# Four of eight blocks of the second MLP product by Strassen's method, accumulators in pairs of banks, fixed product orders

## The chip, the cores and the metric

The kernel runs on one core of a Trainium2 chip. The metric is the device time of one execution in microseconds (us), as the median of several runs. TensorE multiplies matrices and writes its sums to PSUM banks (128 x 512 float32 each, eight of them); VectorE and ScalarE do elementwise work; SP and ScalarE issue the DMAs used here.

## The reference

Two decoder layers over 256 tokens of width 2048. Layer 0 mixes a gated short convolution with differential attention, layer 1 is forgetting attention; each is followed by an MLP with a squared ReLU of hidden width 8192:

```python
def _sqrelu_mlp(h, w1, w2):
    return jnp.square(jax.nn.relu(h @ w1)) @ w2

for l in range(DEPTH):
    h = _rmsnorm(x, norm1_g[l])
    x = x + mixer_l(h)            # layer 0: conv + diff attention; layer 1: forgetting attention
    h = _rmsnorm(x, norm2_g[l])
    x = x + _sqrelu_mlp(h, mlp_w1[l], mlp_w2[l])
```

## The kernel before

**Precision.** Each large product is computed from split operands. A float32 value is cast to a high part (`wh`, or `hi` of an activation, by ScalarE) and VectorE subtracts it from the value to get a low part (`wl`, `lo`). Three matmuls then stand for one product: high by high, high by low, low by high. `split_w` (L142) does this for a weight tile of 1 MB (`raw`, three buffers); `wh` and `wl` have three buffers each (`wspl`, L41).

**Projections.** `gemm` (L153) makes 256 tokens by 512 columns: two accumulators (token halves t), blocks of 512 rows of the weight. Within half a block 12 matmuls are issued in one of six written orders (`ORDERS`, L132), taken in turn. `proj` copies the result out on ScalarE; `out_proj` (L534) adds it to the residual with one VectorE addition for each t. After half a block `step` (L84) advances one generator of `pending`: normalisation, attention, the convolution and `setup` (L246), which loads small parameters on ScalarE's queue, the forget-gate weights `gw` (L260) last.

**The MLP.** `mlp` (L706) goes over four groups g of 2048 hidden units. `hidden` (L604) makes the first product of a group in eight calls of `gemm_t` (L544), 256 hidden units each, 64 matmuls, in one of four orders (`TORDERS`, L699). Its results are taken out later (`take`, L620, put into `late` and run by `flush`), squared, and stored as a pair for the second product. `gemm_pair` (L638) is the second product: it is called twice in a group, for columns n = 0, 1 and n = 2, 3, and each call goes through the eight pairs. A letter of `KINDS` says how a pair is multiplied with its 256 x 1024 block of the weight, seen as a 2 x 2 matrix of blocks:

- C, classical: 8 block products, 24 matmuls; the weight tile is split once.
- S, Strassen's method in Winograd's form: 7 block products, 21 matmuls. VectorE first makes sums of weight blocks (`T`, L650 to L654), and both three of the raw blocks and the four of `T` are split, which takes two of the `wspl` buffers. `PairS.fill` also makes sums of the hidden activations.

In a call, products go to eight PSUM banks: four accumulators (P2, Q3, Q4, X) that S and C share, and P1, Q5, P7, P6 that only S uses. One block behind the last S, those four are combined into `E` and added to the residual (L678 to L689). At the end of the call `final` (L692) adds the four accumulators to the residual, one VectorE operation each, run by the next `flush`. In the last group of the last layer each of the four also starts a store of its 256 KB part of the output.

**Order.** The order in which the engines get their instructions is not the written one: the framework places each instruction when it expects its data and its buffer to be ready, and so pulls instructions ahead of others. On an engine the order is then fixed. A tile of a pool is given again when all that used its buffer before is done.

Of the kernel before, what the change touches and what calls it, by code (L numbers as in the profile page):

```python
# [16 lines left out]
P = 128  # L17
# [9 lines left out]
def trunk_kernel(  # L27
# [18 lines left out]
    accp = ctx.enter_context(tc.tile_pool(name="accp", bufs=4, space=PSUM))  # L46
# [19 lines left out]
    nc.scalar.copy(g1, ps[:, :32])  # L66

# [42 lines left out]
    class ActT:  # L110
# [20 lines left out]

    ORDERS = [  # L132
        lambda kk: [(t, k, p) for t in range(2) for k in kk for p in (0, 1, 2)],
        lambda kk: [(t, k, p) for t in range(2) for k in kk for p in (0, 2, 1)],
        lambda kk: [(t, k, p) for t in range(2) for p in (0, 1, 2) for k in kk],
        lambda kk: [(t, k, p) for k in kk for t in range(2) for p in (0, 1, 2)],
        lambda kk: [(t, k, p) for k in kk for p in (0, 2, 1) for t in range(2)],
        lambda kk: [(t, k, p) for k in kk for p in (0, 1, 2) for t in range(2)],
    ]
    turn = [0, 0]  # L140

# [11 lines left out]
    def gemm(acts, w, c0, first=False):  # L153

        acc = []
        total = 4 * len(acts)
        i = 0
        for ai, a in enumerate(acts):
            raw = wraw.tile([P, 4, CW], F32, name="raw")
            src = w[a.row:a.row + CW, c0:c0 + CW].rearrange("(k p) n -> p k n", p=P)  # L160
            if first and ai == 0:
                for h in range(2):
                    nc.sync.dma_start(raw[:, 2 * h:2 * h + 2, :], src[:, 2 * h:2 * h + 2, :])
            else:
                nc.sync.dma_start(raw, src)
            wh, wl = split_w(raw, parts=2 if first else 1)
            if i == 0:
                flush()
                acc += [accp.tile([P, CW], F32, name="acc") for _ in range(2)]
            until(lambda: a.left <= 0)  # L170
            for h in range(2):
                kk = (2 * h, 2 * h + 1)
                seq = ORDERS[turn[0] % len(ORDERS)](kk)
                for j, (t, k, p) in enumerate(seq):
                    ts = slice(t * P, (t + 1) * P)
                    x = (a.lo if p == 2 else a.hi)[:, k, ts]
                    st = i + 2 * h == 0 and all(q[0] != t for q in seq[:j])
                    sp = i + 2 * h + 2 == total and all(q[0] != t for q in seq[j + 1:])
                    nc.tensor.matmul(acc[t], x, (wl if p == 1 else wh)[:, k, :], start=st, stop=sp)  # L179
                step()  # L180
            i += 4
        turn[0] += 1
        return acc
# [59 lines left out]
    gw = const.tile([P, KT, 16], F32, name="gw")  # L243
    gws = const.tile([P, GP], F32R, name="gws")

    def setup():  # L246
# [13 lines left out]
        nc.scalar.dma_start(gw, fox_w_in[0, :, 3 * D:3 * D + 16].rearrange("(k p) n -> p k n", p=P))  # L260
# [166 lines left out]
    def forget_gates(nm):  # L427

        wv = gws[:, :KT * 32].rearrange("p (k n) -> p k n", n=32)
# [104 lines left out]
    def out_proj(acts, w, nxt):  # L534

        for part in (acts[:-1], acts[-1:]):
            for n in range(NCH):
                acc = gemm(part, w, n * CW)
                for t in range(2):
                    nc.vector.tensor_tensor(xr[n][:, t, :], acc[t], xr[n][:, t, :], ALU.add)  # L540
                if len(part) == 1:
                    pending.append(nxt.chunk(n))

    def gemm_t(acts, w, c0):  # L544
# [3 lines left out]
        for c in range(2):  # L548
# [4 lines left out]
            if c == 0:  # L553
                flush()
                acc += [accp.tile([P, CW], F32, name="acc") for _ in range(2)]
            for h in range(2):
                a = acts[2 * c + h]
                until(lambda: a.left <= 0)
                for f, k, p in TORDERS[turn[1] % len(TORDERS)]:
# [13 lines left out]
    KINDS = "SCSCSCCC"  # L573
# [30 lines left out]
    def hidden(nm, w, c0):  # L604

        pairs, half = [], None
        for i, kind in enumerate(KINDS):
            acc = gemm_t(nm.acts, w, c0 + 2 * i * P)
            if kind == "S":
                p = PairS()  # L610
            elif half is not None:
                p, half = PairC(half), None
            elif "C" in KINDS[i + 1:]:
                t = actp.tile([P, 4, 2, 2 * P], F32R, name="act")
                p, half = PairC(t[:, :2]), t[:, 2:]
            else:
                p = PairC(qkv.tile([P, 2, 2, 2 * P], F32R, name="v"))
# [12 lines left out]
            turn[1] += 1  # L630
# [7 lines left out]
    def gemm_pair(pairs, w, r0, n, r2, done):  # L638
# [3 lines left out]
        for i, (kind, p) in enumerate(zip(KINDS, pairs)):  # L642
# [15 lines left out]
            if i == 0:  # L658
                flush()
                for nm in ("P2", "Q3", "Q4", "X"):  # L660
                    B[nm] = accp.tile([P, CW], F32, name="acc")
# [30 lines left out]
        def final():  # L692
            for bank, m, t in (("P2", n + 1, 0), ("Q3", n, 0), ("X", n, 1), ("Q4", n + 1, 1)):
                nc.vector.scalar_tensor_tensor(
                    xr[m][:, t, :], B[bank], r2[:, t:t + 1], xr[m][:, t, :], ALU.mult, ALU.add)
                done(1, m, t)
        late.append(final)

    TORDERS = [  # L699
        [(f, k, p) for f in range(2) for p in range(2) for k in range(4)],  # L700
        [(f, k, p) for p in range(2) for k in range(4) for f in range(2)],
        [(f, k, p) for p in range(2) for f in range(2) for k in range(4)],
        [(f, k, p) for f in range(2) for k2 in (0, 2) for p in range(2) for k in (k2, k2 + 1)],
    ]
# [97 lines left out]
```

## Time and profile before

| | |
|---|---|
| median of 3 runs | 2183.34 us (2182.51 to 2185.11) |
| profiled execution | 2183.53 us, its span 2181.8 us |
| TensorE busy | 2167.7 us, 10724 instructions |
| VectorE busy | 1541.1 us, 1572 instructions |
| ScalarE busy | 1049.5 us, 1099 instructions |
| read from HBM | 408.28 MB, 188 GB/s over the span |

How to read it: PE is TensorE's matmuls, PEld its weight loads, DVE is VectorE, ACT ScalarE, SP the engine that issues the weight loads; ACTq is ScalarE's queue of instructions. A matmul's row lasts longer than the distance to the next one, since they are pipelined. "<-" names what ended an idle time. L12 is line 12 of the kernel. The span is shorter than the time of the execution by what lies around it.

### The profile page before, as it was taken

How to read it: one execution, taken by the hardware profiler on the slowest of the kernel's cores; microseconds unless marked ns; L12 is line 12 of the kernel's file. 1: busy time of each engine (PE TensorE's matmuls, PEld its weight loads, DVE VectorE, ACT ScalarE, POOL GpSimd, SP SyncE). 2: the span in 40 equal slices, each digit the busy share in tenths (PEclk: the TensorE clock that was granted, in tenths of full speed). 3: DMA queues.
4: the chain of work that ended last, by engine and by line, in shares of the span. 5: the costliest groups of instructions: out<-in, count | busy, mean ns of one | idle time of the engine just before them, and what ended most of it. 6: DMA issues, size and time to landing. Idle time of an engine off the chain costs nothing.

```text
span 2181.8 us, 25989 instructions
## 1 busy us (share of the span) xinstructions
PE 2167.7 (99%) x10724; PEld 1821.4 (83%) x10724; DVE 1541.1 (71%) x1572; ACT 1049.5 (48%) x1099; POOL 17.0 (1%) x17
## 2 busy tenths in 40 slices
PE   8999999999999999999999999999999999999999
PEld 6887888888888888888888888888888888888887
DVE  5576655779768768867856565657797687687687
ACT  6465443544445444445554454445454444444453
POOL 0000000000000000000000000000000000000000
PEclk9999999999999999999999999999999999999999
DMA  7554555555755765665655555556556556656654
GB/s 257 174 174 155 175 191 193 175 172 194 222 182 175 229 191 178 211 193 176 211 173 189 188 176 173 183 174 181 166 205 219 179 181 221 191 186 209 189 189 153
DMA packets 245241, 412.08 MB, mean 189 GB/s; under 512 B 9367, under 2 KB 144770, under 8 KB 245122
## 3 DMA queue, kind: packets, MB, share of 16 engines
q1 hardware_dynamic: 237264, 405.84, 57.4%
q10 hardware_dynamic: 7858, 4.58, 0.7%
q8 instruction: 84, 1.38, 0.3%
q14 instruction: 35, 0.29, 0.0%
HBM read 408.28 MB, written 2.11 MB: 188 GB/s over the span
## 4 chain that ended last, share of the span: by engine, by line
PE 94%; DVE 3%; DMA 2%; ACT 1%; issue 0%; SPq 0%; ACTq 0%; DVEq 0%
PE acc L179 32%; PE acc L562 22%; PE acc L566 11%; PE acc L635 7%; PE acc L636 7%; PE acc L634 7%; PE tp L635 2%; PE tp L634 2%; PE tp L636 2%; DVE wl L150 1%; DMA raw<-in_mlp_w_dram 1%; PE tp L199 1%; ACT wh L149 0%; PE tp L320 0%; DVE qk L651 0%
## 5 line engine op out<-in xcount | busy, mean ns | idle before, releaser
L150 DVE TENSOR_TENSOR wl<-raw,wh 128x2048 fp32r<-128x2048 f32 (+2 forms) x388 | 853.7, 2202 | 507.5 <-ACT wh L149 507.2
L149 ACT CAST wh<-raw 128x2048 fp32r<-128x2048 f32 (+2 forms) x388 | 713.2, 1840 | 758.3 <-issue 249.7
L179 PE MATMUL acc<-wh,act 128*128 128x512 f32 x2048 | 624.2, 398 | 1.7 <-ACT wh L149 1.7
L562 PE MATMUL acc<-act,wh 128*128 128x512 f32 x2048 | 557.6, 394 | 0.0
L179 PEld LDWEIGHTS acc<-wh,act 128*128 128x128 f32 x2048 | 380.8, 189 | 79.3 <-ACT wh L149 2.1
L562 PEld LDWEIGHTS acc<-act,wh 128*128 128x128 f32 x2048 | 349.9, 189 | 45.7 <-DVE act L128 0.6
L179 PE MATMUL acc<-wl,act 128*128 128x512 f32 x1024 | 360.6, 392 | 2.8 <-DVE wl L150 2.8
L566 PEld LDWEIGHTS acc<-act,wl 128*128 128x128 f32 x2048 | 314.3, 189 | 43.4
L566 PE MATMUL acc<-act,wl 128*128 128x256 f32 x2048 | 324.7, 281 | 0.0
L635 PE MATMUL acc<-wl,act 128*128 128x512 f32 x656 | 256.3, 391 | 1.5 <-DVE wl L150 1.4
L636 PE MATMUL acc<-wh,act 128*128 128x512 f32 x656 | 255.3, 389 | 0.0
L634 PE MATMUL acc<-wh,act 128*128 128x512 f32 x656 | 251.5, 389 | 0.0
L179 PEld LDWEIGHTS acc<-wl,act 128*128 128x128 f32 x1024 | 193.0, 189 | 44.3 <-DVE wl L150 4.0
L635 PEld LDWEIGHTS acc<-wl,act 128*128 128x128 f32 x656 | 123.1, 188 | 30.1 <-DVE wl L150 4.7
L634 PEld LDWEIGHTS acc<-wh,act 128*128 128x128 f32 x656 | 123.2, 188 | 25.8
L636 PEld LDWEIGHTS acc<-wh,act 128*128 128x128 f32 x656 | 123.2, 188 | 25.3
L149 ACT CAST wh<-qk 128x2048 fp32r<-128x2048 f32 x48 | 91.9, 1914 | 105.0 <-DVE qk L654 69.6
L150 DVE TENSOR_TENSOR wl<-qk,wh 128x2048 fp32r<-128x2048 f32 x48 | 109.9, 2290 | 22.6 <-ACT wh L149 22.4
L624 ACT COPY qk<-acc 128x256 f32<-128x256 f32 x128 | 43.9, 369 | 73.4 <-PE acc L566 73.4
L635 PE MATMUL tp<-wl,act 128*128 128x512 f32 x192 | 74.8, 389 | 0.0
L634 PE MATMUL tp<-wh,act 128*128 128x512 f32 x192 | 74.7, 389 | 0.0
L636 PE MATMUL tp<-wh,act 128*128 128x512 f32 x192 | 74.7, 389 | 0.0
(171 smaller groups left out, 1424.2 us busy)
## 6 DMA issues: line engine op xcount, KB each, us to landing
raw<-in_mlp_w_dram SPq DMA_DIRECT2D x256, 1024.0 KB, 5.5
raw<-in_fox_w_in_dram SPq DMA_DIRECT2D x48, 1024.0 KB, 5.1
raw<-in_hyb_w_in_dram SPq DMA_DIRECT2D x47, 1024.0 KB, 5.1
raw<-in_hyb_w_out_dram SPq DMA_DIRECT2D x16, 1024.0 KB, 5.1
raw<-in_fox_w_out_dram SPq DMA_DIRECT2D x16, 1024.0 KB, 5.0
ob<-fcd ACTq DMA_DIRECT2D x4, 512.0 KB, 5.7
xr<-in_x_dram SPq DMA_DIRECT2D x3, 512.0 KB, 7.3
raw<-in_hyb_w_in_dram SPq DMA_DIRECT2D x2, 512.0 KB, 5.4
```

The costliest lines, as they stand in the source:

```text
L149: nc.scalar.copy(wh[:, s], src[:, s])
L150: nc.vector.tensor_tensor(wl[:, s], src[:, s], wh[:, s].bitcast(F32), ALU.subtract)
L179: nc.tensor.matmul(acc[t], x, (wl if p == 1 else wh)[:, k, :], start=st, stop=sp)
L199: nc.tensor.transpose(ps[:, t * P:(t + 1) * P], xr[n][:, t, j * P:(j + 1) * P], ident)
L562: nc.tensor.matmul(acc[f], wh[:, 4 * h + k, fs], a.both[:, k, :, :].rearrange("p s t -> p (s t)"), start=c + h + k == 0, stop=False)
L566: nc.tensor.matmul(acc[f][:, 2 * P:], wl[:, 4 * h + k, fs], a.hi[:, k, :], start=False, stop=(c, h, k) == (1, 1, 3))
L624: nc.scalar.copy(fj, acc[j][:, 2 * P:])
L634: nc.tensor.matmul(acc, a[0], b[0], start=not started, stop=False)
L635: nc.tensor.matmul(acc, a[0], b[1], start=False, stop=False)
L636: nc.tensor.matmul(acc, a[1], b[0], start=False, stop=last)
```

## The change

1. `KINDS` goes from `SCSCSCCC` to `SSCSCSCC`: four S instead of three, the first two in a row; E is combined behind block 6 instead of block 5, and one C stands behind that. The hidden pairs of the last two C lie in `qkv`'s `v` buffers.
2. PSUM accumulators are taken in pairs of banks (`acc_pair`): `out_proj` adds both token halves in one operation, `final` has two operations (t = 0, then 1) over two column blocks each, and the next user of a pair waits for all that reads the pair. In the last group the two stores of a t start behind its operation.
3. `gemm` and `gemm_t` use one fixed order each (the fifth of the six, the fourth of the four).
4. At the start eight, and before the first block's matmuls six more, transposes of the identity are issued into a scratch accumulator pair (`idle`); the first weight tile is loaded and split in four pieces instead of two.
5. The forget-gate weights are loaded and split in `forget_gates` of layer 1, into tiles of `work` and `actp`, not in `setup` into tiles of their own.

```diff
-    accp = ctx.enter_context(tc.tile_pool(name="accp", bufs=4, space=PSUM))
+    accp = ctx.enter_context(tc.tile_pool(name="accp", bufs=2, space=PSUM))
...
+    def acc_pair():
+        t = accp.tile([P, 2, CW], F32, name="acc")
+        return [t[:, 0, :], t[:, 1, :], t]
+    def idle(n):
+        scratch = acc_pair()[0]
+        for _ in range(n):
+            nc.tensor.transpose(scratch[:, :P], ident, ident)
+    idle(8)
...
-                for h in range(2):
-                    nc.sync.dma_start(raw[:, 2 * h:2 * h + 2, :], src[:, 2 * h:2 * h + 2, :])
+                for h in range(4):
+                    nc.sync.dma_start(raw[:, h, :], src[:, h, :])
...
-            wh, wl = split_w(raw, parts=2 if first else 1)
+            wh, wl = split_w(raw, parts=4 if first and ai == 0 else 2 if first else 1)
             if i == 0:
                 flush()
-                acc += [accp.tile([P, CW], F32, name="acc") for _ in range(2)]
+                acc += acc_pair()
             until(lambda: a.left <= 0)
+            if first and ai == 0:
+                idle(6)
...
-                seq = ORDERS[turn[0] % len(ORDERS)](kk)
+                seq = [(t, k, p) for k in kk for p in (0, 2, 1) for t in range(2)]
...
+        gt = actp.tile([P, 16 * P], F32R, name="act")
+        gws = gt[:, :GP]
+        gw = work.tile([P, 2 * P], F32, name="y").rearrange("p (k n) -> p k n", n=16)
+        nc.scalar.dma_start(gw, fox_w_in[0, :, 3 * D:3 * D + 16].rearrange("(k p) n -> p k n", p=P))
+        yield
...
-                for t in range(2):
-                    nc.vector.tensor_tensor(xr[n][:, t, :], acc[t], xr[n][:, t, :], ALU.add)
+                nc.vector.tensor_tensor(xr[n], acc[2], xr[n], ALU.add)
...
+    TORDER = [(f, k2 + j, p) for f in range(2) for k2 in (0, 2) for p in range(2) for j in range(2)]
...
-                for f, k, p in TORDERS[turn[1] % len(TORDERS)]:
+                for f, k, p in TORDER:
...
-    KINDS = "SCSCSCCC"
+    KINDS = "SSCSCSCC"
...
-            elif "C" in KINDS[i + 1:]:
+            elif i < 3:
...
-                for nm in ("P2", "Q3", "Q4", "X"):
-                    B[nm] = accp.tile([P, CW], F32, name="acc")
+                B["Q3"], B["P2"], B[0] = acc_pair()
+                B["X"], B["Q4"], B[1] = acc_pair()
...
-            for bank, m, t in (("P2", n + 1, 0), ("Q3", n, 0), ("X", n, 1), ("Q4", n + 1, 1)):
-                nc.vector.scalar_tensor_tensor(
-                    xr[m][:, t, :], B[bank], r2[:, t:t + 1], xr[m][:, t, :], ALU.mult, ALU.add)
-                done(1, m, t)
+            for t in range(2):
+                x2 = xall[:, n:n + 2, t, :]
+                nc.vector.scalar_tensor_tensor(x2, B[t], r2[:, t:t + 1], x2, ALU.mult, ALU.add)
+                for m in (n, n + 1):
+                    done(1, m, t)
```

## Rows read from the trace of the kernel before

**Rows 1.** Page: busy us (share of the span), instructions.

```profile
PE 2167.7 (99%) x10724; PEld 1821.4 (83%) x10724; DVE 1541.1 (71%) x1572; ACT 1049.5 (48%) x1099; POOL 17.0 (1%) x17
```

**Rows 2.** Page: chain that ended last, shares by engine.

```profile
PE 94%; DVE 3%; DMA 2%; ACT 1%; issue 0%; SPq 0%; ACTq 0%; DVEq 0%
```

**Rows 3.** Waits: us in total, times, longest us.

```profile
PEld acc L635 <- DVE wl L150: 4.7, 8, 1.0
```

**Rows 4.** Windows: busy us (instructions) by engine, clock, DMA share, GB/s.

```profile
571.00:660.00 89.00, 89.00 (x512) 78.05 (x511) 59.51 (x60) 39.41 (x39) 0.00 (x0) 1.00 0.61 188
1577.00:1618.00 41.00, 41.00 (x183) 33.95 (x182) 36.47 (x30) 20.32 (x14) 0.00 (x0) 1.00 0.57 198
1618.00:1659.00 41.00, 41.00 (x183) 33.93 (x182) 35.13 (x25) 20.48 (x12) 0.00 (x0) 1.00 0.64 212
```

**Rows 5.** Chain in order of time, 240 to 330 us: start, us, what.

```profile
253.40 57.16 PE acc L179 x252
```

**Rows 6.** Lines by form: count | busy us, mean ns | idle.

```profile
L150 DVE TENSOR_TENSOR wl<-raw,wh 128x2048 fp32r<-128x2048 f32 x332 | 760.7, 2291 | 505.1 <-ACT wh L149 504.8
...
L150 DVE TENSOR_TENSOR wl<-raw,wh 128x1536 fp32r<-128x1536 f32 x48 | 84.0, 1750 | 0.0
...
L694 DVE SCALAR_TENSOR_TENSOR xr<-acc,r,xr 128x512 f32<-128x512 f32 x64 | 44.3, 743 | 5.5 <-PE acc L636 5.5
...
L653 DVE TENSOR_TENSOR qk<-qk,raw 128x512 f32<-128x512 f32 x48 | 33.0, 687 | 0.8
```

**Rows 7.** Timeline of VectorE, 676 to 700 us: start, us, operation, [idle].

```profile
683.18 2.29 DVE L150 TENSOR_TENSOR wl<-raw,wh 128x2048 fp32r<-128x2048 f32 x1 [3.68 <-ACT wh L149]
...
688.80 2.28 DVE L150 TENSOR_TENSOR wl<-raw,wh 128x2048 fp32r<-128x2048 f32 x1
691.00 1.22 DVE L683 TENSOR_TENSOR qk<-tp,qk 128x1024 f32<-128x1024 f32 x1
692.13 1.22 DVE L651 TENSOR_TENSOR qk<-raw 128x1024 f32<-128x1024 f32 x1
693.26 2.47 DVE L688 SCALAR_TENSOR_TENSOR xr<-qk,r,xr 128x1024 f32<-128x1024 f32 x2
```

**Rows 8.** Chain in order of time, 570 to 703 us.

```profile
664.17 6.49 DMA raw<-in_mlp_w_dram
670.75 1.24 DVE qk L651
...
673.35 2.29 DVE wl L150
```

**Rows 9.** Chain in order of time, 703 to 760 us.

```profile
707.04 0.91 PE acc L634 x4
```

**Rows 10.** Timeline of TensorE, 8 to 14 us.

```profile
8.36 1.22 PE L179 MATMUL acc<-wh,act 128*128 128x512 f32 x2 [1.66 <-ACT wh L149]
...
11.50 0.63 PE L179 MATMUL acc<-wh,act 128*128 128x512 f32 x1
11.92 0.63 PE L179 MATMUL acc<-wl,act 128*128 128x512 f32 x1
...
13.37 0.60 PE L199 MATMUL tp<-ident,xr 128*128 128x128 f32 x4
```

**Rows 11.** Windows at the start.

```profile
10.00:20.00 10.00, 10.00 (x45) 8.08 (x45) 5.12 (x8) 7.06 (x15) 0.00 (x0) 1.00 1.05 392
36.00:43.00 7.00, 4.30 (x12) 2.97 (x13) 6.49 (x7) 6.46 (x9) 0.00 (x0) 0.77 0.46 150
```

**Rows 12.** Timeline of ScalarE, 36 to 43 us.

```profile
38.38 1.26 ACT L230 ACTIVATE qk<-acc,rstd 128x512 f32<-128x512 f32 x2
...
42.53 0.41 ACT L431 CAST gws<-gw 128x256 fp32r<-128x256 f32 x1
```

**Rows 13.** Timeline of TensorE, 34 to 44 us.

```profile
38.70 0.50 PE L179 MATMUL acc<-wl,act 128*128 128x512 f32 x1 [2.79 <-DVE wl L150]
```

**Rows 14.** Chain in order of time, 26 to 45 us.

```profile
28.25 7.39 DMA ob<-in_hyb_lk_dram
```

More of the change, by code (lines that the diff above doesn't have):

```diff
@@ L129, in split @@
             self.left -= n
[L132 to L140, printed above, removed]
     def split_w(src, shape=(4, CW), parts=1):
@@ L181, in gemm @@
             i += 4
-        turn[0] += 1
         return acc
@@ L242, in trunk_kernel @@
     GP = 16 * 32 + 96
-    gw = const.tile([P, KT, 16], F32, name="gw")
-    gws = const.tile([P, GP], F32R, name="gws")
     def setup():
@@ L259, in setup @@
         nc.scalar.dma_start(bfb, fox_b_f.broadcast_to([P, 16]))
-        nc.scalar.dma_start(gw, fox_w_in[0, :, 3 * D:3 * D + 16].rearrange("(k p) n -> p k n", p=P))
         nc.gpsimd.memset(mask, 0.0)
@@ L554, in gemm_t @@
                 flush()
-                acc += [accp.tile([P, CW], F32, name="acc") for _ in range(2)]
+                acc += acc_pair()
             for h in range(2):
@@ L629, in hidden @@
             late.append(take)
-            turn[1] += 1
         return pairs
@@ L692, in final @@
         def final():
-            for bank, m, t in (("P2", n + 1, 0), ("Q3", n, 0), ("X", n, 1), ("Q4", n + 1, 1)):
-                nc.vector.scalar_tensor_tensor(
-                    xr[m][:, t, :], B[bank], r2[:, t:t + 1], xr[m][:, t, :], ALU.mult, ALU.add)
-                done(1, m, t)
-        late.append(final)
[L699 to L704, printed above, removed]
+            for t in range(2):
[3 more added lines that the diff above has]
+                    done(1, m, t)
+        late.append(final)
     def mlp(nm, l, nxt):
```

## The prediction

> **What bounds the kernel now.** I read the page's busy shares first: TensorE is busy 99% of the span, VectorE 71% [rows 1]. The chain that ended last says the same: 94% of it is TensorE [rows 2]. So time is won by issuing fewer matmuls, and lost where another engine makes TensorE wait. Next I read the waits. Within the second MLP product the one that counts is a weight load waiting for a low part (`wl`, VectorE): 4.7 us in 8 places of the whole span [rows 3]. Then the stretches: in a stretch of the first product VectorE is busy 59.5 of 89 us; in the two calls of `gemm_pair` behind another one it is busy 36.5 and 35.1 of 41 us, with TensorE at 41.0 [rows 4]. The margin of VectorE in `gemm_pair`, some 13%, is what this change spends.
>
> The sum is made against the profiled execution's 2183.53 us (span 2181.8, about 1.7 around it). It stands 0.2 above the median of the runs, 2183.34, so I carry the result over unchanged.
>
> **The change part by part.**
>
> *Fewer products.* `KINDS` goes from three S and five C to four and four. S is 7 products of 3 matmuls (21), C is 8 (24). A call falls from 183 to 180 matmuls; there are 16 calls (2 layers, 4 groups, 2 column pairs), so 48 matmuls go. Their price is the pitch at which they follow each other: 252 matmuls of this form took 57.16 us, 0.2268 each [rows 5]. 48 x 0.2268 = **-10.9 us**, all on the path.
>
> *VectorE's price of an S.* The durations stand in [rows 6, 7]; back to back each follows the last some 0.08 us before its row ends (688.80 to 691.00, 691.00 to 692.13 [rows 7]), so I use pitches. An S needs three additions (1.14 + 0.61 + 0.61) and two low parts (1.67 + 2.21): 6.2 us. A C needs one low part: 2.2. Difference 4.0 per call; the final's two operations over two banks (I take 1.25 each, from the 1024-wide one in [rows 7]) for four of 0.66 give back 0.1 to 0.2. For a group's two calls: before, 71.6 us of VectorE under 2 x 183 x 0.2268 = 83.0 of TensorE, 11.4 idle; after, 79.3 under 81.6, **2.3 idle**. So VectorE does not become the bound by its sum, but its present idle time must nearly all be filled. ScalarE's one more cast is covered (20.4 busy of 41 [rows 4]); the extra vector operations of an S fill lie in the stretches of the first product, where VectorE has 29.5 us idle of 89 [rows 4]; without that cover they would cost some 1.5 us a group (an estimate from the additions' rows).
>
> *Where it gets tight.* Let x be the end of the last S block in a group's first call. The queue behind it: the combination E (0.6 + 0.6 + 1.13 + two adds in 2.4 = 4.7), low part of the last C (2.2), S0 of the second call (6.2), the final (2.5), and now S1 (6.2): VectorE is done at x+21.8. TensorE runs two C after x (before: three), 5.44 each: S0 starts at x+10.9, S1 at x+15.6. The last low part of S1 feeds only 4 of its 21 matmuls; if the others go first it is wanted at x+15.6+3.9 = x+19.5, 2.3 too early. If TensorE also takes the 16 high-part matmuls of the following C first, at x+23.1, 1.3 to spare. The order on the engines is not the written one: four high products in a row stand at 707.04 [rows 9], so such postponing happens already. By the same count the old order had S0 at x+16.3, and its queue needed 15.3 before it. Hand-overs between engines come on top, and a load is late by more than the order expects: the S addition at 670.75 waited for a load of 6.49 us, and a C's low part queued behind it until 673.35 [rows 8]. VectorE also stood idle for 3.68 us just before x, waiting for a cast whose buffer was still in use [rows 7]; with three `wspl` buffers and four needed by S S, some such gaps stay. At the start of the first call S S is easier: the first S can be prepared ahead, as now.
> Price of the waits: at least what eight perfect groups give, 0; at most 3.4 us a group, if half of the 11.4 idle stays. I take 1.0 a group, 8.0 in all, near the middle of 0 and 2.3: against the 4.7 of now **+3.3 us**.
>
> *Start.* The first twelve matmuls run at 0.42 us (11.50 to 11.92), about twice 0.2268, so I read them as run at the lower clock level, 1.2 GHz; 8.36 to 13.37 is 5.0 us for what takes 2.7 at the upper [rows 10]. The added transposes fill TensorE ahead of 8.36 us, and loads and casts come in quarters (the two more issues stand on SP's queue ahead of the next chunk of x, which the first block's 5.4 us cover). Gain at most 2.3 (3.3 if it also begins 1 us earlier); but the loads run at 392 GB/s with a share of 1.05 there [rows 11], so the next block waits for its megabyte; I take -1.8.
> The Trainium skill ("TensorE: Matmul & The Clock Gate", Part 4: PE-mode transpose) says transposes do not count as activity that raises the clock. No row before shows a stretch of transposes alone, so the trace does not decide it; it is the fourth rival.
> The second idle takes the accumulator pair between the first two projections, so the second uses the first one's pair and waits for its two copies. Those ran at 38.38 to 39.64 [rows 12], while TensorE resumed at 38.70 after a wait of 2.79 [rows 13]: +0.9 (0 to 2). That wait comes from a small load of 7.39 us [rows 14]; the gate weights leave that queue: -0.4 (0 to -4.8, should the wait and the low clock behind it, 0.77 in 36 to 43 us [rows 11], vanish). Start **-1.3**, bounds -8 to +3.
>
> *Gate weights later.* The load now stands in `forget_gates`, and ScalarE's casts behind it wait for it. Before, those casts ran at 42.4 us [rows 12], a whole layer ahead of their use, so instructions are pulled forward when their buffers allow. 0 to 4.8 (what the like load cost TensorE at the start, 2.79 [rows 13], and the low clock behind it); nearest to hidden, **+0.3**.
>
> *End.* The last final is one operation over two banks and then two stores on one queue, where now one of 0.74 us [rows 6] and one store stand behind the last matmul. 1.3 for 0.74, and up to half a microsecond of issue (an estimate): **+0.7** (0 to 1).
>
> *Nothing:* the fixed orders. The 252 matmuls of [rows 5] run through three of the six lists, the kept one among them, without a difference; the first product's 512 matmuls fill their 89 us under all four lists [rows 4]. Projection adds in one instruction instead of two of the same length together. Releasing accumulators in pairs lies beside other work, 0 to 0.2 us a call.
>
> Sum: -10.9 + 3.3 - 1.3 + 0.3 + 0.7 = -7.9, **2175.6 us**.
>
> **Rivals.**
> 1. *Everything is hidden* (waits 0.1 a group). For it: the margin of 1.3 with postponing, and only 4.7 us of such waits now. Against: 2.3 idle left of 11.4. -10.9 + 0.8 - 4.7 - 0.3 = -15.1: 2168.4.
> 2. *The gain turns into waits* at S1 of the second call, 2.0 a group, as the 2.3 without postponing past the block: -10.9 + 16 - 4.7 - 0.3: 2183.6, no change.
> 3. *VectorE becomes the bound, slower.* Half of the idle time stays (5.7 a group), because buffers, not work, make it: 79.3 + 5.7 - 81.6 = 3.4 a group, 27.2 in all: +11.3, 2194.8. It decides from 2.0 us of wait a group upward, that is from 4.3 us of VectorE idle time kept. For it: the 3.68 gap, and a backlog with no C between two S; against: old gaps lie partly where VectorE is ahead.
> 4. *The added transposes do not raise the clock*, and the first block keeps its 0.42 us pitch but for smaller first pieces: 1.4 of the start's gain goes, 2177.0.
>
> **How the numbers follow.** Forecast 0.38, everything hidden 0.13, the transposes 0.10: faster 0.61. No change 0.21. Slower 0.18. A change of 0.2%, 4.4 us, is about the least that can be told from none. The forecast's own range is 2170 to 2179 (waits 0.3 to 1.4 a group). Eight in ten: from rival 1, with a start a little better, 2167, to close under rival 3, 2193.
>
> **What would show it.** Products of L634's kind 960 for 976. VectorE in a stretch of `gemm_pair` busy near 39 to 40 of 41. Low-part waits at the blocks after the second call's first S: about 1 us a group right, over 2 wrong. First matmuls at 0.23 instead of 0.42 us. If VectorE's busy time per call rose by much less than 4 us, or TensorE waited for casts rather than low parts, the mechanism is wrong even with the right time.

## The result: 3.25% slower

The changed kernel takes 2254.20 us (median of 5 runs, 2253.22 to 2254.72); the kernel before took 2182.51 in 5 runs beside it. The ratio is 1.0325 [1.0313, 1.0338] (in brackets the 95% interval, here and below), +71.7 us. The forecast was 2175.6 with a range of 2167 to 2193, so both sign and range were missed.

The profiled execution's span went from 2181.8 to 2252.5 us, +70.7. Cut at the first matmul of each stretch on TensorE's timeline, it divides so: the eight stretches of the second product +74.5, the two of projections -2.4, the eight of the first product -1.3. Within the +74.5, 48 matmuls fewer give -10.9, as forecast; the waits and slow matmuls in the products (what each block took above its count x 0.2267 us) rise from 4.0 to 86.9; the tail behind the last matmul grows by 1.3; some 1.2 lies at other ends of stretches.

The page of the changed kernel, busy time and chain, answers to [rows 1, 2]: the 48 matmuls are gone (10724 - 48 + 14 transposes = 10690), and VectorE's part of the chain that ended last rises from 3% to 13%.

```profile
PE 2189.7 (97%) x10690; PEld 1813.1 (80%) x10690; DVE 1613.1 (72%) x1614; ACT 1074.3 (48%) x1117; POOL 16.2 (1%) x17
...
PE 80%; DVE 13%; DMA 3%; ACT 2%; issue 2%; ACTq 0%; SPq 0%; DVEq 0%
```

The waits of the changed kernel (us in total, times, longest), to be held against [rows 3]:

```profile
ACT wh L151 <- DVE qk L661: 211.6, 40, 8.1
...
PEld tp L641 <- ACT wh L151: 29.7, 16, 2.9
PEld tp L642 <- DVE wl L152: 27.1, 32, 2.1
...
PE tp L641 <- ACT wh L151: 22.9, 16, 2.5
...
PE tp L642 <- DVE wl L152: 15.1, 10, 1.7
...
PE acc L570 <- DVE xr L702: 8.6, 6, 1.4
```

The first of them stood so in the kernel before:

```profile
ACT wh L149 <- DVE qk L654: 69.6, 23, 5.8
```

Read them from the top: ScalarE's cast of the sums (`wh`) waits for VectorE's last addition (L661), up to 8.1 us; TensorE's high products (L641, accumulators `tp`: those only S uses) wait for that cast; and the low products for the low parts. The last row is another matter: the next first product waits for the final, which holds the accumulators.

Taken by block over the 16 calls, 60.2 of the 86.9 us lie at block 1, the second S, and 54.6 of these in the eight second calls of a group: 6.3 to 7.3 each. 9.5 lie at the ends of the groups. S0 and S1 below are the first and the second S of a call (in the changed kernel its blocks 0 and 1).

One such place in full, the second call of the group that starts at 665.29. The call starts at 708.47. VectorE's timeline, its queue from the last low parts of the first call on (start, us, operation):

```profile
697.46 0.68 DVE L688 TENSOR_TENSOR qk<-tp,qk 128x512 f32<-128x512 f32 x1
698.06 2.28 DVE L152 TENSOR_TENSOR wl<-raw,wh 128x2048 fp32r<-128x2048 f32 x1
...
703.72 2.47 DVE L695 SCALAR_TENSOR_TENSOR xr<-qk,r,xr 128x1024 f32<-128x1024 f32 x2
...
709.58 2.28 DVE L152 TENSOR_TENSOR wl<-qk,wh 128x2048 fp32r<-128x2048 f32 x1
711.78 1.28 DVE L702 SCALAR_TENSOR_TENSOR xr<-acc,r,xr 128x1024 f32<-128x1024 f32 x1
712.97 1.21 DVE L658 TENSOR_TENSOR qk<-raw 128x1024 f32<-128x1024 f32 x1
714.11 1.75 DVE L152 TENSOR_TENSOR wl<-raw,wh 128x1536 fp32r<-128x1536 f32 x1
715.77 0.68 DVE L660 TENSOR_TENSOR qk<-qk,raw 128x512 f32<-128x512 f32 x1
716.38 1.22 DVE L658 TENSOR_TENSOR qk<-raw 128x1024 f32<-128x1024 f32 x1
717.51 0.68 DVE L661 TENSOR_TENSOR qk<-qk,raw 128x512 f32<-128x512 f32 x1
...
720.23 2.29 DVE L152 TENSOR_TENSOR wl<-qk,wh 128x2048 fp32r<-128x2048 f32 x1 [0.71 <-ACT wh L151]
```

No row from 697.46 to 718.83 has an idle time: E, a C's low part, S0, the finals and S1 stand in one line. Nor is it a buffer that S1 waits for: its sums can take E's as soon as E's additions (L695) are done, at 706.2 (in e12 below they start right there). S1's additions begin only at 712.97 and end at 718.2, with the first sum of the call's third S (716.38) let in ahead. ScalarE has waited for them, and its cast for the following C stands behind that one:

```profile
718.30 1.90 ACT L151 CAST wh<-qk 128x2048 fp32r<-128x2048 f32 x1 [8.10 <-DVE qk L661]
720.11 3.27 ACT L151 CAST wh<-raw 128x2048 fp32r<-128x2048 f32 x2
```

And TensorE, whose S1 was due at 713.6 (start of the call, the 21 matmuls of S0 and 0.4 of waits among them):

```profile
715.91 0.50 PE L642 MATMUL tp<-wl,act 128*128 128x512 f32 x1 [1.66 <-DVE wl L152]
...
717.40 0.40 PE L643 MATMUL acc<-wh,act 128*128 128x512 f32 x1
720.25 0.97 PE L641 MATMUL tp<-wh,act 128*128 128x512 f32 x3 [2.46 <-ACT wh L151]
...
722.07 0.79 PE L641 MATMUL acc<-wh,act 128*128 128x512 f32 x1 [0.62 <-ACT wh L151]
722.66 0.71 PE L642 MATMUL tp<-wl,act 128*128 128x512 f32 x1
723.17 0.63 PE L643 MATMUL tp<-wh,act 128*128 128x512 f32 x1
723.60 0.63 PE L642 MATMUL tp<-wl,act 128*128 128x512 f32 x1
```

The wait of 1.66 is for S1's first low part, that of 2.46 for the cast of the sums. From 722.66 on the matmuls follow each other at 0.43 to 0.51 us: the granted clock has fallen to its lower level, 1.2 GHz, as the windows of this stretch show (the column before the last two is the clock):

```profile
718.00:722.00 4.00, 1.20 (x4) 0.67 (x4) 3.26 (x4) 3.70 (x3) 0.00 (x0) 1.00 0.66 201
722.00:726.00 4.00, 3.93 (x10) 3.04 (x11) 4.00 (x3) 1.38 (x2) 0.00 (x0) 0.57 0.28 78
```

Such a stretch of half clock, some 3.4 us long (once twice that), stands behind S1 of every group's second call. In windows of the same cut as [rows 4], VectorE is not full over the calls:

```profile
577.00:666.00 89.00, 89.00 (x512) 77.59 (x512) 60.15 (x61) 38.89 (x37) 0.00 (x0) 1.00 0.60 187
666.00:708.00 42.00, 40.80 (x176) 32.61 (x175) 36.88 (x31) 20.95 (x16) 0.00 (x0) 1.00 0.52 176
708.00:751.00 43.00, 38.17 (x157) 29.98 (x156) 36.31 (x26) 20.54 (x13) 0.00 (x0) 0.96 0.55 175
```

It has 5.1 and 6.7 us of idle time in the two windows, but none in the 21 us that decide.

### The profile page after: what moved, and what is told of

Same layout as the page of the kernel before. It is cut to its first block, busy times and chain, and to the rows that moved or that the text cites. A ratio compares the mean times of both kernels' runs of the same rounds, so it can differ in the third digit from the quotient of the medians.

```text
span 2252.5 us, 26045 instructions
## 1 busy us (share of the span) xinstructions
PE 2189.7 (97%) x10690; PEld 1813.1 (80%) x10690; DVE 1613.1 (72%) x1614; ACT 1074.3 (48%) x1117; POOL 16.2 (1%) x17
## 4 chain that ended last, share of the span: by engine, by line
PE 80%; DVE 13%; DMA 3%; ACT 2%; issue 2%; ACTq 0%; SPq 0%; DVEq 0%
PE acc L184 30%; PE acc L570 21%; PE acc L574 10%; DVE wl L152 6%; PE acc L642 4%; PE acc L643 4%; PE acc L641 4%; DMA raw<-in_mlp_w_dram 2%; ACT wh L151 2%; DVE qk L658 2%; DVE xr L702 1%; PE tp L642 1%; PE tp L643 1%; DVE xr L695 1%; PE tp L641 1%
## 5 line engine op out<-in xcount | busy, mean ns | idle before, releaser
L152 DVE TENSOR_TENSOR wl<-raw,wh 128x2048 fp32r<-128x2048 f32 (+3 forms) x390 | 844.1, 2168 | 445.8 <-ACT wh L151 445.4
L151 ACT CAST wh<-raw 128x2048 fp32r<-128x2048 f32 (+3 forms) x390 | 704.7, 1814 | 644.1 <-PE acc L184 239.5
L570 PE MATMUL acc<-act,wh 128*128 128x512 f32 x2048 | 644.3, 396 | 8.6 <-DVE xr L702 8.6
L184 PE MATMUL acc<-wh,act 128*128 128x512 f32 x2048 | 565.6, 397 | 1.4 <-DVE xr L702 0.8
L574 PEld LDWEIGHTS acc<-act,wl 128*128 128x128 f32 x2048 | 384.7, 188 | 90.8
L184 PEld LDWEIGHTS acc<-wh,act 128*128 128x128 f32 x2048 | 375.9, 188 | 77.8 <-issue 3.0
L574 PE MATMUL acc<-act,wl 128*128 128x256 f32 x2048 | 402.5, 278 | 0.0
L570 PEld LDWEIGHTS acc<-act,wh 128*128 128x128 f32 x2048 | 311.9, 189 | 11.2 <-issue 10.9
L184 PE MATMUL acc<-wl,act 128*128 128x512 f32 x1024 | 318.7, 391 | 0.6 <-DVE wl L152 0.6
L641 PE MATMUL acc<-wh,act 128*128 128x512 f32 x448 | 177.0, 400 | 2.5 <-ACT wh L151 2.5
L642 PE MATMUL acc<-wl,act 128*128 128x512 f32 x448 | 177.1, 395 | 2.1 <-DVE wl L152 2.1
L643 PE MATMUL acc<-wh,act 128*128 128x512 f32 x448 | 175.6, 392 | 0.0
L641 PE MATMUL tp<-wh,act 128*128 128x512 f32 x256 | 93.9, 409 | 22.9 <-ACT wh L151 22.9
L641 PEld LDWEIGHTS acc<-wh,act 128*128 128x128 f32 x448 | 85.8, 192 | 27.9 <-ACT wh L151 9.3
L643 PE MATMUL tp<-wh,act 128*128 128x512 f32 x256 | 103.5, 404 | 0.0
L641 PE MATMUL acc<-wh,v 128*128 128x512 f32 x256 | 99.7, 389 | 0.0
```

Of the source, the lines that this page charges most:

```text
L151: nc.scalar.copy(wh[:, s], src[:, s])
L152: nc.vector.tensor_tensor(wl[:, s], src[:, s], wh[:, s].bitcast(F32), ALU.subtract)
L570: nc.tensor.matmul(acc[f], wh[:, 4 * h + k, fs], a.both[:, k, :, :].rearrange("p s t -> p (s t)"), start=c + h + k == 0, stop=False)
L574: nc.tensor.matmul(acc[f][:, 2 * P:], wl[:, 4 * h + k, fs], a.hi[:, k, :], start=False, stop=(c, h, k) == (1, 1, 3))
L641: nc.tensor.matmul(acc, a[0], b[0], start=not started, stop=False)
L642: nc.tensor.matmul(acc, a[0], b[1], start=False, stop=False)
```

## Experiments

Theory A: VectorE's queue behind the last S of a group's first call is too long for the two C that cover it, so S1 comes late. Rival B: the `wspl` buffers make it late. Rival C: the accumulators in pairs of banks hold TensorE. All ratios are against the kernel before, run on the same chip (medians 2183.6 to 2184.6). "Waits" are again the time of the product's blocks above 0.2267 us a matmul, over all 16 calls: 4.0 before, 86.9 after.

### First: number, order, banks

**e1: three S, all else as changed.**

```diff
-    KINDS = "SSCSCSCC"
+    KINDS = "SCSCSCCC"
-            elif i < 3:
+            elif "C" in KINDS[i + 1:]:
```

> The changed kernel with three S blocks again (SCSCSCCC); all its other parts stay (pairs of banks, fixed orders, start, gate weights). Theory A (the fourth S and the two S in a row overload VectorE's queue at the second call of a group): all of the 9.4 us a group goes and the start's 3.4 us stay won: 2177 to 2183. Rival C (the pairs of banks hold TensorE up): the waits at the second call stay in part and the time stays above 2195.

2196.70 us, 1.0060 [1.0043, 1.0077]; waits 20.3. So 57.5 of the 71.7 us go with the fourth S in this order, but the rest of the change, without it, is still a loss of 13. The time lies in rival C's range and not in theory A's: both have a part, which e4 and e8 size.

**e2: four S, taken in turn with C** (`KINDS = "SCSCSCSC"`).

> The changed kernel with four S blocks, each followed by one C (SCSCSCSC). Theory A as a matter of place (two S right behind the combination E): the wait of 6.7 us at the second S goes; E now stands behind the last block, so one of 2 to 4 us a group takes its place at the first S of the second call: 2190 to 2210. Theory A as a matter of sum (VectorE's work for four S does not fit): the loss stays, above 2235.

2263.24 us, 1.0364 [1.0343, 1.0385], the slowest of all; waits 76.6. With one C behind the last S, E stands before the finals: 29.0 us of the waits are the next first product waiting for the final, 41.9 lie at S0, 36.8 of them in the second calls (4.6 a group where 2 to 4 were expected). The time is in the range of "a matter of sum"; e3, with the same work in another order, shows that the sum is not the cause.

**e3: the neighbouring S put late** (`KINDS = "SCSCSSCC"`).

> Four S blocks, the two in a row as the third and fourth S, two C last (SCSCSSCC). Theory A by place: no S pair stands behind E, so the wait is 1 to 3 us a group at the S pair: 2185 to 2205. By sum: above 2235. If the two S in a row are the cause wherever they stand (buffers: four wanted, three there): near 2254.

2198.80 us, 1.0069 [1.0049, 1.0089]; waits 30.7. Two S in a row are not dear in themselves: with a C between S0 and S1 of the second call, 56 us of the waits go.

**e4: single banks, four S in the order of the change.** Short form of the edit; `out_proj` and `final` go back to one operation for each bank too.

```diff
-    accp = ctx.enter_context(tc.tile_pool(name="accp", bufs=2, space=PSUM))
+    accp = ctx.enter_context(tc.tile_pool(name="accp", bufs=4, space=PSUM))
...
-                B["Q3"], B["P2"], B[0] = acc_pair()
-                B["X"], B["Q4"], B[1] = acc_pair()
+                for nm in ("P2", "Q3", "Q4", "X"):
+                    B[nm] = accp.tile([P, CW], F32, name="acc")
```

> The changed kernel (SSCSCSCC) with four single accumulators, four final operations and two additions in the output projection as before. Theory A: only the wait of 1.6 us between the second product and the next first product goes, six times, and some tenths elsewhere: 2240 to 2247. Rival C (pairs of banks): below 2200.

2233.46 us, 1.0228 [1.0207, 1.0248]; waits 69.6, of which 55.0 at block 1. Pairs cost 20.7 us here, more than the 7 to 14 of theory A's range, but the wait at S1 stays with single banks: rival C is not its cause. In the waits the pairs show as 17.3 us: 11.2 at blocks 1 to 3 of the first calls, 3.0 each at block 4 of the second calls and at the ends of the groups, where 6.6 stay. TensorE's timeline in the same group, every row with an idle time between 690 and 730 us:

```profile
712.43 0.50 PE L642 MATMUL tp<-wl,act 128*128 128x512 f32 x1 [1.53 <-DVE wl L151]
716.77 0.97 PE L641 MATMUL tp<-wh,act 128*128 128x512 f32 x3 [2.67 <-ACT wh L150]
718.58 1.16 PE L641 MATMUL acc<-wh,act 128*128 128x512 f32 x3 [0.61 <-ACT wh L150]
```

### Second: what in the queue makes S1 late

**e5: e3's order with single banks** (e4 with `KINDS = "SCSCSSCC"`).

> Four S blocks with the pair late (SCSCSSCC) and single accumulators. If the two costs add up as in the runs so far (pairs of banks 14 to 20 us, the place of the S pair some 55), it takes the 17 us or so off the 2198.8 of the same order with pairs: 2176 to 2184, that is the 48 matmuls and the start won and little else lost. If single accumulators help only where S S stands behind E: 2194 to 2200.

2198.32 us, 1.0069 [1.0052, 1.0085], as e3: the two costs do not add up. In this order single banks win nothing. The waits (33.3) are hardly fewer anywhere: 17.1 at the first three blocks of the second calls (e3: 16.9), 7.6 at the ends of the groups (9.5), and 8.0 at block 3 of the first calls, where e3 has none but 3.8 at their S0. What pairs cost depends on the order of the blocks; by what steps was not taken apart.

**e6: the changed kernel without the three additions** of T. The four sums are left out and the split takes raw blocks in their place, so casts, low parts, the buffers of `wspl` and the products stay in number and size.

```diff
-                T = qkv.tile([P, 4, CW], F32, name="qk")
-                nc.vector.tensor_tensor(
-                    T[:, 0:2], raw[:, 1:3], raw[:, 0:1].broadcast_to([P, 2, CW]), ALU.add)
-                nc.vector.tensor_tensor(T[:, 2], T[:, 1], raw[:, 1], ALU.add)
-                nc.vector.tensor_tensor(T[:, 3], T[:, 2], raw[:, 3], ALU.add)
-                wa, wb = split_w(raw[:, 1:4]), split_w(T)
+                wa, wb = split_w(raw[:, 1:4]), split_w(raw)
```

> The changed kernel without the three VectorE additions of each S (the second split takes the raw tile instead of the sums); buffers, matmuls and order of blocks stay. Theory A (VectorE's queue and the sums at its end make S1 late): the wait of 6 to 7 us at the second call's second S falls under 1 us: 2180 to 2200, the pairs of banks still paid. Rival B (four wspl buffers wanted, three there): the wait stays, above 2235.

2182.50 us, 0.9996 [0.9985, 1.0006]: 71.7 us less than the changed kernel for 2.4 us of additions an S. Waits 15.6; at the second calls' S1 0.1 a group. Of TensorE's waits for another engine (us in total, times, longest) the release of the pairs is now the largest, and those for low parts are small:

```profile
PE acc L570 <- DVE xr L697: 8.9, 6, 1.8
...
PEld tp L642 <- DVE wl L152: 3.5, 14, 0.3
```

The buffers of `wspl` are asked for just as before, and the wait is gone: rival B falls. The additions act twice, by their own time in the queue and because ScalarE's cast must wait for the last of them; this run takes both away, and their buffers (`qk`, two in number) with them.

**e7: the changed kernel without E** (ScalarE's copy of P1, the three instructions that make E and the two additions to the residual are left out; the sums stay).

```diff
-                E = qkv.tile([P, 4, CW], F32, name="qk")
-                nc.scalar.copy(E[:, 3], B["P1"])
-                nc.vector.tensor_tensor(E[:, 2], B["P6"], E[:, 3], ALU.add)
-                nc.vector.tensor_tensor(E[:, 1], B["P7"], E[:, 2], ALU.add)
...
-                    nc.vector.scalar_tensor_tensor(x2, e, r2[:, t:t + 1], x2, ALU.mult, ALU.add)
```

> The changed kernel without the combination E and its two additions to the residual (they are left out). If the length of VectorE's queue behind the last S makes the wait, its 4.7 us are gone and the wait at S1 of the second call falls from 6.7 to 2 or less: 2195 to 2220. If it is the chain of one S alone (sums, cast, low part, one behind the other) that is too long with no C before it, the wait stays within 1 us of what it was: above 2240.

2193.24 us, 1.0044 [1.0028, 1.0060], a little under the range. The wait at the second calls' S1 is 0.17 a group here too, with sums and casts in place. So it is the place in the queue: 4.7 us taken off ahead of S1 are enough. The waits left (27.6) lie elsewhere, as 0.71 a group at the first calls' S1 and 0.85 at their third S.

**e8: three S and single banks** (e4 with e1's edit): the kernel before with the new start, the moved gate weights and the fixed orders.

> Three S blocks as before (SCSCSCCC) and single accumulators: what is left of the change is the start, the gate weights and the fixed orders. If the pairs of banks make the whole 13 us of the three-S run and nothing else costs: 2178 to 2181 (the start's 3 to 4 us won). If the fixed orders cost as well: 2184 to 2192.

2178.04 us (9 runs), 0.9975 [0.9965, 0.9985]; waits 3.5. With e1 and e4 this parts the loss: three S with pairs against single banks, 2196.70 - 2178.04 = 18.7 us; four S in this order against three, both with single banks, 2233.46 - 2178.04 = 55.4, which is -10.9 of matmuls and +66.1 of waits (69.6 - 3.5). From 2178.04, 55.4 for the order and 20.7 for the pairs (2254.20 - 2233.46) make the changed kernel.

### Third: can four S be had

**e9: S S C S S C C C, single banks** (e4 with `KINDS = "SSCSSCCC"`): one C more behind the last S.

> Four S blocks as SSCSSCCC with single accumulators: three C after the last S, as before, so E and the second call's first S are covered, but S S comes straight behind them. By the queue behind E (4.7 + 4.4 + 6.2 + 2.6 + 6.2 = 24.1 us, the second S's products wanted about 1.5 us earlier): a wait of 1 to 2 us a group at S1, 1 us at the second pair, none before the first product: 2175 to 2190. If S S at the front costs as much as in the change whatever stands before it: above 2220.

2188.78 us (10 runs), 1.0021 [1.0012, 1.0030]; waits 26.5, 21.8 of them at the second calls' S1. The extra C (5.4 us) takes off 4.2 of e4's 6.9 us a group. Its rows there have shorter waits, and no half clock behind them in the group shown:

```profile
705.87 0.97 PE L641 MATMUL tp<-wh,act 128*128 128x512 f32 x3 [0.95 <-ACT wh L150]
707.67 0.96 PE L641 MATMUL acc<-wh,act 128*128 128x512 f32 x3 [0.60 <-ACT wh L150]
```

In seven of the eight groups it is so. In the sixth the same two waits (0.95 and 0.60) were followed by 3.4 us of half clock, and its S1 lost 3.8 us where the others lost 2.6:

```profile
1801.00:1804.40 3.40, 3.40 (x9) 2.58 (x9) 3.40 (x3) 1.12 (x1) 0.00 (x0) 0.50 0.11 43
```

**e10: S C S S C S C C, single banks** (`KINDS = "SCSSCSCC"`).

> Four S blocks as SCSSCSCC with single accumulators: a C between E's backlog and the S pair, but only two C after the last S. By the queue: about the 2198 of SCSCSSCC, 2190 to 2202, with the wait of 1.1 to 1.3 us at the end of each group again, since E stands one block before the end. By the sum of VectorE's work alone, no difference to the other orders of four S with a late pair: the same.

2198.61 us, 1.0063 [1.0043, 1.0083]; waits 33.6, 12.1 of them at the first of the two neighbouring S in the second calls, 8.9 at the ends of the groups. A C between S0 and S1 makes the wait smaller (1.5 a group) and leaves others.

**e11: e8 without the fourteen transposes** (`idle(8)` and `idle(6)` taken out).

> The three-S kernel with single accumulators (2178.0) without the fourteen added transposes. If transposes raise TensorE's clock: the first granted full clock comes at about 12.5 us instead of 8.6, and the time is 1.5 to 3 us longer, 2179.5 to 2181. If they do not count: the clock rises at the same time with and without them, and the time stays within 0.5 us.

2178.08 us (7 runs), 0.9972 [0.9961, 0.9984], the same as e8, though the clock differs: e8's is at its upper level from 6.65 us on, e11's from 13.07, with its first matmuls at 0.42 us. Both halves of what was expected missed: the transposes do raise the clock, but no gain shows in the time. e8 waits 1.37 us for a load of x, up to 12.36 us, and reaches the first product 0.9 us before e11 (392.78 against 393.66 us), less than the spread of e8's runs (2176.19 to 2179.44). In e8 the clock rises while TensorE has done nothing but transposes, and their own distance falls from 0.21 to 0.11 us (start, us, operation):

```profile
2.95 1.97 PE L76 MATMUL acc<-ident 128*128 128x128 f32 x8
...
6.88 0.82 PE L76 MATMUL acc<-ident 128*128 128x128 f32 x6
7.45 1.17 PE L183 MATMUL acc<-wh,act 128*128 128x512 f32 x4
```

**e12: e4 with S1's three additions on GpSimd, in both calls.**

```diff
+                add = nc.gpsimd if i == 1 else nc.vector
-                nc.vector.tensor_tensor(
+                add.tensor_tensor(
...
```

> The changed order (SSCSCSCC) with single accumulators, 2233.5, and the three sums of the second S of each call on GpSimd instead of VectorE. By theory A, VectorE's queue is 2.4 us shorter there and the sums can be made ahead: the wait at S1 of the second call falls from 6.7 to 2 to 4 us: 2195 to 2215. If GpSimd and VectorE take turns at the SBUF, VectorE's rows beside it become longer and the gain is eaten: 2225 or more.

2234.52 us, 1.0227 [1.0207, 1.0247], no gain over e4; waits 67.5. The second calls' S1 falls from 6.9 to 1.6 a group, but the first calls' S1 rises from 0 to 3.3 and the second calls' S0 from 0.4 to 1.9. The sums keep their buffers here and only change the engine, so the fall at that S1 speaks for the queue once more. GpSimd's additions are long, and VectorE's rows beside them grow (lines by form: count, busy us, mean ns):

```profile
L151 DVE TENSOR_TENSOR wl<-qk,wh 128x2048 fp32r<-128x2048 f32 x64 | 159.0, 2485 | 64.3 <-ACT wh L150 64.3
L151 DVE TENSOR_TENSOR wl<-raw,wh 128x1536 fp32r<-128x1536 f32 x64 | 123.3, 1926 | 14.8 <-ACT wh L150 14.8
...
L659 POOL TENSOR_TENSOR qk<-raw 128x1024 f32<-128x1024 f32 x16 | 53.7, 3358 | 1742.0 <-DVE wl L151 1444.7 <-DVE xr L696 297.2
```

The means hide that few rows pay: 8 of the 64 low parts of sums take 3.8 us, the other 56 keep 2.3. One of the eight, and GpSimd's additions beside it (start, us, operation); it takes 1.6 us more than alone, and GpSimd's first addition ends 1.7 us after its start, as if the two took turns:

```profile
707.26 3.85 DVE L151 TENSOR_TENSOR wl<-qk,wh 128x2048 fp32r<-128x2048 f32 x1
...
704.64 4.31 POOL L659 TENSOR_TENSOR qk<-raw 128x1024 f32<-128x1024 f32 x1 [37.60 <-DVE xr L696]
709.03 3.22 POOL L661 TENSOR_TENSOR qk<-qk,raw 128x512 f32<-128x512 f32 x1
```

### Fourth: the best of both

**e13: e9 with S1's additions on GpSimd in the second call only** (e12's edit with `i == 1 and n == 2`).

> SSCSSCCC with single accumulators (2188.8) and the three sums of the second S made by GpSimd, in the second call of a group only. Theory A: its wait of 2.6 us at that S is VectorE's queue, so it shrinks, while the first call, where GpSimd's 7.6 us came too late, keeps VectorE: 2170 to 2182, the first four-S kernel at or under the three-S one's 2178. If every gain there comes back as VectorE's longer rows beside GpSimd: 2186 to 2192.

2180.72 us (11 runs), 0.9986 [0.9977, 0.9995]; waits 17.0. At S1 0.44 us a group are left of e9's 2.72, and S0 (0.79) and the third S (0.28) are a little late. It is the fastest kernel with four S, and still 2.7 us above e8 with three: against it, 10.9 us of matmuls are won and 13.5 of waits lost.

**e14: e8 with the gate weights loaded in `setup` again.**

```diff
+    gw = const.tile([P, KT, 16], F32, name="gw")
+    gws = const.tile([P, GP], F32R, name="gws")
...
+        nc.scalar.dma_start(gw, fox_w_in[0, :, 3 * D:3 * D + 16].rearrange("(k p) n -> p k n", p=P))
```

> The three-S kernel with single accumulators (2178.0) with the gate weights' load and split in setup again, as before. If the moved load makes the start's gain: the low-part wait near 35 us comes back, 2.8 us and a stretch of low clock behind it, and the time is 2180.5 to 2183. If the smaller first pieces and the fixed order make it: within 0.5 us of 2178.0.

2176.74 us, 0.9967 [0.9955, 0.9979], against 2178.04 and 0.9975 [0.9965, 0.9985] for e8, measured on another chip. The intervals overlap and the wait near 35 us does not come back: no gain from moving that load shows.

**e16: S C S S S C C C, single banks** (e8 with `KINDS = "SCSSSCCC"`, `elif i < 3`).

> Four S blocks as SCSSSCCC with single accumulators: three C behind the last S and one C between the first S and the next three. By the queue: no wait at the second call's first S, but three S in a row need 18.6 us of VectorE in 14.3 of TensorE with two buffers for their sums: 2 to 4 us a call at the third and fourth S: 2195 to 2225. If only the place behind E matters: 2172 to 2180.

2197.64 us, 1.0063 [1.0045, 1.0081]; waits 34.4, none at the second calls' first three S, 24.6 at the last, the third in a row, and 7.8 at block 3 of the first calls. Three C behind the last S clear the queue; three S in a row fill it again.

**e17: the kernel before with the fixed orders alone.**

```diff
-                seq = ORDERS[turn[0] % len(ORDERS)](kk)
+                seq = ORDERS[4](kk)
...
-                for f, k, p in TORDERS[turn[1] % len(TORDERS)]:
+                for f, k, p in TORDERS[3]:
```

> The kernel before with the fixed orders of products and nothing else. The prediction priced them at nothing: 2182 to 2184. If they make what the three-S kernels win (2177 to 2178), because the low parts come last in the first two projections: 2177 to 2180, and the wait of 2.8 us near 35 us is gone.

2177.93 us (11 runs), 0.9977 [0.9968, 0.9986], as e8. So the orders alone win as much as e8 does. More than half of it comes from one place near 36 us. Where [rows 13] had a wait of 2.79 us for a low part and [rows 11] a clock of 0.77, this kernel waits 0.47 and keeps the clock:

```profile
37.18 0.73 PE L179 MATMUL acc<-wl,act 128*128 128x512 f32 x2 [0.47 <-DVE wl L150]
```

```profile
36.00:43.00 7.00, 6.53 (x29) 4.75 (x28) 6.87 (x11) 6.03 (x9) 0.00 (x0) 1.00 0.69 231
```

Its first stretch of projections takes 384.79 us for 388.35; six of the first-product stretches take 89.16 for 89.42 (89.25 with pairs). Why that low part comes earlier was not taken apart.

**e18: e9 with only the widest of S1's additions on GpSimd in the second call.**

> SSCSSCCC with single accumulators and only the first and widest sum of the second call's second S on GpSimd (with all three: 2180.7). If GpSimd's slow second and third sums hold that S up: 2174 to 2179. If the rows of VectorE that become longer beside GpSimd are the cost: 2180 to 2186.

2192.32 us, 1.0042 [1.0028, 1.0056], slower than e9 and above both ranges. VectorE's next addition waits for GpSimd's, 4957 ns long on the mean, and holds all behind it; 19.9 us of waits appear at S0.

## Why the prediction was wrong, step by step

**The step that failed is "Price of the waits ... I take 1.0 a group", with "at most 3.4".** Measured: (86.9 - 4.0) / 8 = 10.4 a group. It was wrong in three ways.

1. *It let only the low part be late.* "The last low part of S1 feeds only 4 of its 21 matmuls; if the others go first it is wanted at ... x+19.5." But the sums need three additions and then ScalarE's cast before any of their products can run. Nine of S1's 21 matmuls work on raw blocks; the other twelve need that cast or the low part behind it. With x at 697.6 (start of the first call plus 132 matmuls and its waits) S1 was due at x+16.0, as forecast (x+15.6). The additions were done at x+20.6, the cast at x+22.6, the last low part at x+24.9. TensorE had nine matmuls to bridge this. The following C's high products, which the prediction let go first for its "1.3 to spare", could not help: their cast stands behind that of the sums (720.11). The queue's length itself was nearly right: done at x+21.8 by forecast, three late, 1.1 of it the sum of the third S let in ahead of S1's last addition.
2. *It gave the wait no consequence.* Behind 1.66 and 2.46 us of waiting the granted clock fell, in all eight groups, and matmuls after it followed at 0.43 us; seven or eight of some 0.2 us too much in the group shown, about 1.5 us. The prediction saw this itself at the start of the kernel [rows 10, 11] and did not carry it to its own waits. In e9, with waits of 0.95 and 0.60, it fell in one group of eight.
3. *It averaged the margin over two calls.* "2.3 idle" of a group was a sum; VectorE did keep idle time (11.8 of the two windows' 85 us; the sign "near 39 to 40 of 41" did not come, it was 36.9 of 42 and 36.3 of 43), outside the stretch that decides, and had none in it. e6 and e7 show it: 2.4 us an S, or 4.7 us once a call, less in that queue, and the wait goes.

**Rival 3 named the mechanism**, "a backlog with no C between two S", and 10.4 us of wait a group lie far past its turning point of 2.0. Its price, 3.4 a group, came from idle time kept, not from the cast behind the additions, and was too low by 7.

**"Releasing accumulators in pairs ... 0 to 0.2 us a call" was wrong.** With three S they cost 18.7 us (e1 against e8), 1.2 a call. A pair's final starts when both banks are complete, and the next user waits for the whole read. What shows of it: the first product behind a group waits 1.59 us in the changed kernel, of which 1.10 stay with single banks (e4) and so belong to the order; 0.34 in e1, nothing in e8. In e1, S0 of the first calls takes 0.48 too long, blocks 1 and 3 of the second calls 0.8 each, where e8 has nothing at these; by which steps the pairs make the latter late was not taken apart. With e3's order they cost nothing that shows, with the order of the change 20.7.

**"Nothing: the fixed orders" was wrong the other way**: they win 5.7 us (2177.93 against 2183.61). The 252 matmuls of [rows 5] ran in several orders without a difference; [rows 13] show a place where a low part was late, and there the order made one.

**Start.** Forecast -1.3; the first stretch of projections is 3.4 us shorter. e17 puts this to the orders (its stretch is 3.6 shorter); of the transposes and the gate weights no gain shows in the time (e11, e14; forecast for the moved load: +0.3). The first matmuls of the changed kernel, but for the very first, do run at 0.23 us (start, us, operation):

```profile
7.17 1.49 PE L77 MATMUL acc<-ident 128*128 128x128 f32 x6
8.30 1.32 PE L184 MATMUL acc<-wh,act 128*128 128x512 f32 x4
9.46 0.62 PE L184 MATMUL acc<-wl,act 128*128 128x512 f32 x2
```

The clock reaches its upper level at 8.63 us here and at 6.65 in e8, without the transposes at 12.51 (before) and 13.07 (e11). So rival 4 falls, and "the next block waits for its megabyte" was right in kind: what takes part of the gain away in e8 is a wait for a load, of x. The rule behind rival 4 (the Trainium skill, "TensorE: Matmul & The Clock Gate", Part 4: PE-mode transpose), by which transposes do not count, is not borne out by these float32 transposes; whether they run in the mode that the page means, the rows, which call them MATMUL, do not say. The trace of the kernel before holds a stretch of transposes alone too, eight from 4.67 to 6.70 us with a wait of 1.66 behind them, and the clock stayed low there.

**Right:** the matmuls, -10.9, 960 products of each kind as forecast; VectorE's price of an S (its busy time rose by 72.0 us, 4.5 a call, with what the S adds in the first product; forecast 4.0). The end was sized at +0.7 and took +1.3, above its bound of 1 (from the last matmul to the end of the span 5.44 us for 4.11). That "TensorE waited for casts rather than low parts" was named as what would make the mechanism wrong: it waited for both, the longer time for the cast.

**A version that beats both kernels:** three S, single banks, fixed orders: 2177.93 (e17), 2178.04 (e8), 2176.74 (e14), 0.23 to 0.33% under the kernel before; these three can't be told apart. None of the six orders of four S that ran, with pairs or single banks, with or without GpSimd, came below it. Whether another order of the written instructions would let four S win is open.

## What to carry to other kernels

When a change spends an engine's idle time, follow its queue through the tightest stretch, item by item, to each hand-over that another engine needs (additions, then the cast, then the high product), and not to its last item alone; an average margin over the stage says nothing. A wait on TensorE is priced with what follows it: where rows show the clock at half behind such a wait, add that, as a chance where it comes in some places only. Before two buffers are joined into one, ask who waits for the first half.

## What the runs showed of the hardware that was not expected

- Transposes of 128x128 float32 raised the granted clock: it was at its upper level from 6.65 us, ahead of the first other matmul at 7.45 (e8), and from 13.07 us without the added ones (e11).
- The clock fell in eight groups of eight behind two waits of 1.66 and 2.46 us with seven matmuls between them, in one of eight behind 0.95 and 0.60 (e9), and in three of eight behind 1.34 (once 1.12) and 0.61 (e16, its fourth S). Equal waits in equal code did not always have the same end.
- An addition of 1024 columns takes 1.22 us on VectorE; on GpSimd its rows, which are rough, say 2.4 us in e12's first calls, 4.3 in its second and 5.0 in e13. Of the 64 low parts of sums, the 8 beside them take 3.8 us in e12 and 3.3 to 3.4 in e13; the others keep 2.3.
